# A hybrid gMLP and sparse-attention block on one core: top-k rounds placed elsewhere on VectorE, one low part made by another engine, one softmax behind a split, operands at new addresses

## The chip, the cores and the metric

The kernel runs on one core of one Trainium2 chip. The metric is the device time of one execution in microseconds (us). A core has five engines that run side by side and wait for each other only at semaphores: TensorE (PE in the profile; PEld is its loading of the stationary operand), VectorE (DVE), ScalarE (ACT), GpSimd (POOL) and SyncE (SP), which here only starts DMAs. DMA moves data between main memory and the core's buffer; one kind, started by POOL, adds to what lies at the target.

## The reference

One decoder layer on x of 512 x 1024, all in fp32. The block modulates a normalized x, projects it once, and splits the result:

```python
h = rms_norm(x, norm1_g) * (1.0 + scale1) + shift1
z = h @ w_in     # -> a_u, a_v, q, k, v, qi, ki, wi, g_a, g_b
y_a = chunked_gmlp(gelu(a_u), gelu(a_v), ...)        # mixer A: 128 x 128 causal mixing in 8 groups
score = sum_h wi * relu(qi @ ki.T)                   # indexer, causal
sel_score, sel_idx = lax.top_k(score, 128)           # per query: 128 keys
y_b = attention(q, k, v over the selected keys)      # mixer B: 8 heads, 2 kv heads
merged = sigmoid(g_a) * (y_a @ w_proj_a) + sigmoid(g_b) * (y_b @ w_proj_b)
x = x + gate1 * (merged @ w_out)
x = x + gate2 * swiglu(norm2(x) modulated)           # FFN, then a last RMSNorm
```

## The kernel before

**Products.** Every fp32 product is made of three fp32r matmuls, high·high, high·low and low·high (`mm3`, L53 to L55). So each weight chunk (128 x 1024, 512 KB) that SP streams in as `raw` is split: ScalarE writes its rounded copy `hi` (L128), and the low part `lo` comes in one of two ways. Either VectorE subtracts, raw − hi (L135), or, where the chunk is marked "dma", ScalarE writes the rounded −raw into `lo` (L130) and POOL starts a DMA that adds raw to it (L131). Activations are split in the same way by ScalarE (L379) and VectorE (L380).

**Order.** There is no scheduler: each engine executes its instructions in the order in which the code issues them. The stages are: norm 1 with the k projection and the first q chunks (to 53 us); the rest of q and the indexer's projections (to 109); W_AV, eight steps `vs` (to 160); W_AU, eight steps s = 0 to 7, two chunks W_AU[g][0] and W_AU[g][1] per group g (to 211); then four times a gate unit (`ga_unit(g)`, two steps) and the two chunks of W_PA[g], s = 8 to 23 (to 298); attention, with the chunks of W_GB between its steps (to 384); W_PB, W_O, the FFN.

**Names.** In the W_AU and gate steps `au_tasks` issues what VectorE and ScalarE do beside the matmuls. `mix_mm` forms a mixing product in a PSUM bank `mix`; `mix_a` (L1014, L1017) and `mix_b` (L379, L380) turn it into y and split y. A gate unit multiplies sums and differences of weight and activation blocks (`pga`); the low parts of its weight combinations are subtracted by VectorE (L1088). `part<-pb,sg` (L1185) takes a W_PA product out of PSUM. The row sums L233 (`Gc`) are short side products of other weights. `t_diff_h(n)` forms differences of blocks of the activation, `hraw`, and `t_split_h(n)` splits them; the tables QT and VT say in which step of the q and W_AV stages these are issued, behind the indexer's scores (`idx`, `rl`, `sco`).

**Top-k.** Selecting 128 keys takes 16 rounds for each of three query blocks i = 3, 2, 1 (block 0 has no more than 128 keys). A round is `topk_round(i)`: MAX8 finds the eight largest (L749), MATCH_REPLACE strikes them out (L750); after the sixteenth, `topk_end` (L753) makes the mask. The rows are 512, 384 and 256 wide. The 48 rounds and three ends wait in the list `bg`; `run_bg(us)` adds `us` to a credit and issues rounds while it lasts, each priced at 0.65 + 0.26·i (at most 1.5 is carried over). What an attention unit still needs is issued ahead of its softmax.

**Attention.** A unit u is one query block and one pair of heads; the twelve units go by in steps. In step s, `at_step(s)` issues the product of unit s−3's weights with v (`pv`), the scores of unit s (`qk`), its softmax (`at_soft_a`, L1221 and L1223), the transposes of unit s−2 (`pT`, L1254) with the split of the transposed weights into `th` (ScalarE, L1309) and `tl` (VectorE, L1310), and the second half of the softmax of unit s−1 (L1238, L1240). Unit 8 is the first of block 1; the pool `mid` gives tiles their addresses in the order of their first declaration.

Of the kernel before, what the change touches and what calls it, by code (L numbers as in the profile page):

```python
# [9 lines left out]
F32 = mybir.dt.float32  # L10
# [18 lines left out]
def block_kernel(ctx: ExitStack, tc: tile.TileContext, x, positions, w_ada_t, w_in,  # L29
# [3 lines left out]
    T, V, A, P, SY = nc.tensor, nc.vector, nc.scalar, nc.gpsimd, nc.sync  # L33
# [5 lines left out]
    w_in, w_ffn_in, w_ffn_out = w_in[0], w_ffn_in[0], w_ffn_out[0]  # L39
# [152 lines left out]
    hraw = base.tile([128, 128 + 4096], F32, name="hraw", tag="s2b", bufs=1)  # L192
# [12 lines left out]
        return base.tile([128, 1024], F32R, name=name, tag=f"S2_{k}", bufs=1)[:, :]  # L205
    mid_stack = ExitStack()
    mid = mid_stack.enter_context(tc.tile_pool(name="mid", bufs=1))
    mv = mid.tile([128, 4, 2], F32, name="mv")
    mva = mid.tile([128, 4, 2], F32, name="mva")
    for t in ("v_hi", "v_lo"):  # L210
        mid.tile([128, 1024], F32, name="eraw", tag=t, bufs=1)
    bst = mid.tile([128, 4, 24], F32, name="bst")
    mid.tile([128, 16], F32, name="fill2")
    ffn = []
# [24 lines left out]
    def group(src, c0, n=256, K=8, mods=None, dma=(), where=None, nm=1, mraw="A2"):  # L239
        ids = []  # L240
        for k0 in range(0, K, 4):
            ids.append(add_w(src, list(range(k0, min(K, k0 + 4))), c0, n,
                             "dma" if k0 // 4 in dma else V, where.pop(0) if where else None))
            for _ in range(nm if isinstance(nm, int) else nm[k0 // 4]):
                m = next(mods, None) if mods is not None else None
                if m is not None:
                    add_m(*m, mid=mods is mm_ and mraw)
                    if mraw == "A2" and mods is mm_:
                        stream[-1]["mid"] = ("A2", "G0")[mid2[0] % 2]
                        mid2[0] += 1  # L250
        return ids
# [31 lines left out]
                addm("A2" if k % 4 else "A1")  # L283
    W_AU = []
    for g in range(4):
        W_AU.append(group(w_in, 256 * g, dma=(0, 1) if g else ()))
        if g in (1, 2):
            addm("A2" if g == 1 else "G0")
    W_GA, W_PA = [], []
# [65 lines left out]
    for i in range(4):  # L355
        t = base.tile([128, D], F32, name=f"x{i}", tag=f"X{i}", bufs=1)
# [42 lines left out]
    ch(lambda: V.tensor_scalar(ang, ang, 3.1415925, -3.1415925, op0=OP.min, op1=OP.max))  # L399
    ch(lambda: V.scalar_tensor_tensor(nl, ang, -1.0, ang, op0=OP.mult, op1=OP.max))  # L400
    ch(lambda: V.tensor_scalar(nl, nl, -1.0, math.pi / 2, op0=OP.mult, op1=OP.add))
    sn = mid.tile([128, 4, 128], F32, name="sn", tag="A2", bufs=1)
    tab = {"i": mid.tile([128, 2, S], F32, name="tab_i", tag="G2", bufs=1),
           "q": mid.tile([128, 2, S], F32, name="tab_q", tag="G3", bufs=1)}
# [221 lines left out]
    def q_rope(G):  # L626
        rope_a(("q", G), qpk[G], "q", 128)

    def q_roped(G):
        rope_b(("q", G))  # L630
        for k in range(4):
            h = 4 * G + k
            P.dma_start(qdv[h // 2][0:32, h % 2], qpk[G][32 * k:32 * k + 32].rearrange("p (i n) -> p i n", i=4))
# [23 lines left out]
    k_hi = mid.tile([128, 2, S], F32R, name="k_hi", tag="k_hi", bufs=1)  # L657
# [9 lines left out]
    v_lo = mid.tile([128, 4, 256], F32R, name="v_lo", tag="v_lo", bufs=1)  # L667
    kit = mid.tile([128, 4, 64], F32, name="kit", tag="A1", bufs=1)
    kin = mid.tile([128, 4, 128], F32, name="kin", tag="A2", bufs=1)
    wi = mid.tile([128, 4, 8], F32, name="wi")  # L670
    mid.tile([128, 96], F32, name="fill")
    rki = sm[:, 8:12]

    def ki_stats():
# [93 lines left out]
    def run_bg(us):  # L768
        credit[0] += us
        while bg and credit[0] >= bg[0][0] and iu[1] >= 8 * (4 - bg[0][1]):  # L770
            pop_bg()
        credit[0] = min(credit[0], 1.5)
# [47 lines left out]
    def idx_mms(n):  # L820
        while iu[0] < 24 and n:
            idx_mm(units[iu[0]])
            iu[0] += 1
            n -= 1

    qstep = [0, 0]
    QT = {0: [lambda: k_a(0)],
          1: [lambda: k_a(1), lambda: rope_b(("k", 0))],
# [4 lines left out]
          6: [lambda: qi_b(3, 1), lambda: qi_b(3, 0)],  # L833
          7: [ki_stats, lambda: k_b(0), ki_norm],
          8: [lambda: k_b(1)],
          9: [lambda: q_rope(0)], 10: [lambda: q_roped(0)]}

    def q_tasks():
        s = qstep[0]
# [79 lines left out]

    TH = {}  # L920

    def hblk(kh, th):
        return hraw[:, kh * 2048:(kh + 1) * 2048].rearrange("p (j n) -> p j n", j=4)[:, :, th * 256:(th + 1) * 256]

    def t_diff_h(n):
        b11, b21, b12, b22 = (hblk(kh, th) for th in range(2) for kh in range(2))
        V.tensor_sub(*{1: (b11, b12, b11), 3: (b12, b22, b12), 2: (b22, b22, b11), 4: (b21, b21, b22)}[n])

    def t_split_h(n):
        src = {1: hblk(0, 0), 3: hblk(0, 1), 2: hblk(1, 1), 4: hblk(1, 0)}[n]  # L930
        if n == 3:
            hi = base.tile([128, 4, 256], F32R, name="th_", tag="gate", bufs=1)
            lo = [mid.tile([128, 256], F32R, name="tl_", tag=t, bufs=2) for t in ("qh", "qh", "ql", "ql")]
            A.activation(hi, src, AF.Copy)
            for j in range(4):
                V.tensor_sub(lo[j], src[:, j], f(hi[:, j]))
            TH[3] = ([hi[:, j] for j in range(4)], lo)
        elif n < 4:
            t = [base.tile([128, 4, 256], F32R, name="th_", tag=f"X{2 * n - 2 + e}", bufs=1) for e in range(2)]
            split(*t, src)  # L940
            TH[n] = tuple([t[e][:, j] for j in range(4)] for e in range(2))
        else:
            mid.tile([128, 112], F32, name="fillc")
            hi = mid.tile([128, 4, 256], F32R, name="th_", tag="T4", bufs=1)
            mid.tile([128, 16], F32, name="filld")
            lo = [base.tile([128, 2, 256], F32R, name="tl_", tag="acc", bufs=2) for _ in range(2)]
            A.activation(hi, src, AF.Copy)
            for e in range(2):
                V.tensor_sub(lo[e], src[:, 2 * e:2 * e + 2], f(hi[:, 2 * e:2 * e + 2]))
            TH[4] = ([hi[:, j] for j in range(4)], [lo[j // 2][:, j % 2] for j in range(4)])  # L950

    def hb(kh, th):
        return tuple([s1(8 * e + 4 * kh + j)[:, th * 256:(th + 1) * 256] for j in range(4)] for e in range(2))

    VT = {0: [lambda: t_diff_h(1), lambda: t_diff_h(3)], 1: [lambda: q_rope(1), wn_sums],
          2: [lambda: q_roped(1), lambda: t_diff_h(2)], 3: [lambda: t_split_h(3), lambda: t_diff_h(4)],
          4: [lambda: t_split_h(1), load_bs], 5: [lambda: t_split_h(4)], 6: [lambda: t_split_h(2)], 7: [ws_mask]}
    for i in (3, 2, 1):
        for _ in range(16):
            bg.append((0.65 + 0.26 * i, i, topk_round))  # L960
# [7 lines left out]
    for h in range(2):  # L968
        pb = [bank(b, "pav") for b in range(4)]
        for i in W_AV[h]:  # L970
            idx_accs()
            for fn in VT.get(vs, []):
                fn()
            if vs > 1:
                run_bg(1.2)
            if vs in (5, 6):
                for tk in (2 * vs - 10, 2 * vs - 9):
                    v_stats(tk, 0)
            vs += 1
            hi, lo = get(i)  # L980
            for tk in range(4):
                opt_a_mm(pb[tk], tk, hi, lo, stream[i]["kts"], hT, 8)
            idx_mms(3)
            if vs == 7:
                rows_T()
        for tk in range(4):
            A.activation(vg[tk // 2][:, tk % 2, h * 512:h * 512 + 512], pb[tk], AF.Gelu_apprx_tanh)
# [47 lines left out]
    def au_tasks():  # L1035
        s = austep[0]
        austep[0] += 1
        if s == 0:
            for tk in range(4):
                ln_v(tk)  # L1040
            rstd(rva, mva[:, :, 1], 4)
            V.scalar_tensor_tensor(sm[:, 32:36], mva[:, :, 0], -1.0, rva, op0=OP.mult, op1=OP.mult)
        elif s == 1:
            bias_b()
        if s == 10:
            mix_a(7)
            mix_b(7)
        if s in (6, 10, 14, 18):
            adv(W_GA[(s - 6) // 4][0])
        if s in (7, 11, 15, 19):  # L1050
            ga_b((s - 7) // 4)
        ms = AT.get(s - 1, []) if s < 10 else []
        for m in ms:
            mix_a(m)
        if s > 9:
            run_bg(1.25)
        while dl:
            dl.pop(0)()
        for m in ms:
            mix_b(m)  # L1060
        if 0 < s < 10:
            run_bg(4.0 if s < 6 else 1.25)
        if s == 19:
            at_req(0)
        if s == 22:
            st["stop"] = 1 << 30
# [229 lines left out]
    def at_step(s):  # L1296
        if s >= 3:
            yh, yl, pp = at_pv(s - 3)
            A.activation(yh, pp, AF.Copy)
            V.tensor_sub(yl, pp, f(yh))  # L1300
        if s < NU:
            at_qk(s)
            if s not in (2, 3):
                at_soft_a(s)
            if s == 0:
                at_split(2)
        if 2 <= s <= NU + 1:
            for o, ol, p in at_T(s - 2):
                A.activation(o, p, AF.Copy)  # L1309
                V.tensor_sub(ol, p, f(o))  # L1310
        if s in (2, 3):
            at_soft_a(s)
        if 1 <= s <= NU:
            at_soft_b(s - 1)
        if s < NU:
            at_exp(s)
        if 0 < s < NU - 2 and s != 2:
            at_split(s + 2)
        if 3 < s < 8:
            run_bg(1.0)  # L1320

    for g in range(4):
        ga_unit(g)
# [819 lines left out]
```

## Time and profile before

| what | value |
|---|---|
| runs | 804.96, 804.35, 802.96 us (median 804.35) |
| the profiled execution | 803.53 us; its span 801.5 us |
| mean granted TensorE clock over the span | 0.996 |
| busy: PE, DVE, ACT, POOL | 97%, 84%, 56%, 13% |
| DMA | 148.83 MB, mean 186 GB/s |
| low parts by accumulating DMA | 13, landing 4.4 to 9.6 us after issue |

The span is what the trace covers; the execution's own time is 2 us longer. A busy share is a mean over the whole span. Rows of a timeline give the start in us, the duration, the engine, the line, the operation, output and inputs by the program's names, shapes, and in brackets how long the engine had stood idle before it and which instruction ended that.

### The profile page before, as it was taken

How to read it: one execution, taken by the hardware profiler on the slowest of the kernel's cores; microseconds unless marked ns; L12 is line 12 of the kernel's file. 1: busy time of each engine (PE TensorE's matmuls, PEld its weight loads, DVE VectorE, ACT ScalarE, POOL GpSimd, SP SyncE). 2: the span in 40 equal slices, each digit the busy share in tenths (PEclk: the TensorE clock that was granted, in tenths of full speed). 3: DMA queues.
4: the chain of work that ended last, by engine and by line, in shares of the span. 5: the costliest groups of instructions: out<-in, count | busy, mean ns of one | idle time of the engine just before them, and what ended most of it. 6: DMA issues, size and time to landing. Idle time of an engine off the chain costs nothing.

```text
span 801.5 us, 12714 instructions
## 1 busy us (share of the span) xinstructions
PE 780.9 (97%) x4836; PEld 701.9 (88%) x4836; DVE 675.6 (84%) x1143; ACT 449.2 (56%) x759; POOL 100.9 (13%) x161
## 2 busy tenths in 40 slices
PE   6999999989999999989999999999999999999996
PEld 5789888878889988878888899999999999888886
DVE  6959868987998879997696878899898989887786
ACT  5654556464543365555635577555565556757552
POOL 2082152120000010101000021111111200000001
PEclk9999999999999999999999999999999999999999
DMA  9956487776434443637640608797989876566552
GB/s 356 337 160 176 142 250 228 220 163 182 125 106 132 132 132 112 164 102 260 210 159 1 210 19 211 208 273 229 264 237 245 257 217 168 174 209 190 189 174 105
DMA packets 89485, 148.83 MB, mean 186 GB/s; under 512 B 6992, under 2 KB 56912, under 8 KB 89264
## 3 DMA queue, kind: packets, MB, share of 16 engines
q1 hardware_dynamic: 75056, 106.54, 41.1%
q0 software_dynamic: 12784, 36.97, 19.7%
q10 hardware_dynamic: 1584, 4.50, 1.6%
q8 instruction: 38, 0.62, 0.3%
q14 instruction: 23, 0.19, 0.1%
HBM read 135.80 MB, written 25.17 MB: 201 GB/s over the span
## 4 chain that ended last, share of the span: by engine, by line
PE 61%; issue 13%; DVE 13%; DMA 6%; ACT 4%; POOL 1%; POOLq 0%; DVEq 0%; ACTq 0%
PE R L53 6%; PE R L55 6%; PE R L54 6%; PE pb L55 4%; PE pb L53 4%; PE pb L54 4%; DMA raw<-in_w_ffn_in_dram 3%; PE pfo L54 3%; PE pfo L53 3%; PE pfo L55 3%; PE po L53 2%; PE po L55 2%; PE po L54 2%; PE pgb L53 1%; PE pgb L55 1%
## 5 line engine op out<-in xcount | busy, mean ns | idle before, releaser
L128 ACT ACTIVATE hi<-raw 128x1024 fp32r<-128x1024 f32 (+2 forms) x89 | 92.1, 1039 | 44.9 <-PE pfo L55 18.2
L135 DVE TENSOR_TENSOR lo<-raw,hi 128x1024 fp32r<-128x1024 f32 (+2 forms) x69 | 83.6, 1215 | 31.6 <-ACT hi L128 31.5
L55 PE MATMUL pb<-s,lo 128*128 128x512 f32 (+1 forms) x128 | 48.3, 378 | 2.4 <-DMA lo<-raw 2.4
L54 PE MATMUL pb<-s2b,hi 128*128 128x512 f32 x128 | 49.8, 389 | 0.0
L53 PE MATMUL pb<-s,hi 128*128 128x512 f32 (+1 forms) x128 | 48.6, 379 | 0.0
L54 PE MATMUL pb<-s,hi 128*128 128x512 f32 (+1 forms) x128 | 48.1, 376 | 0.0
L53 PE MATMUL R<-tb,hi 128*128 128x256 f32 x160 | 44.4, 277 | 0.2 <-ACT R L1887 0.2
L53 PE MATMUL R<-tb,sx 128*128 128x256 f32 x160 | 44.3, 277 | 0.2 <-ACT R L1887 0.2
L54 PE MATMUL R<-tb,hi 128*128 128x256 f32 x160 | 44.2, 276 | 0.0
L55 PE MATMUL R<-tb,lo 128*128 128x256 f32 x160 | 44.2, 276 | 0.0
L55 PE MATMUL R<-tb,sx 128*128 128x256 f32 x160 | 44.2, 276 | 0.0
L54 PE MATMUL R<-tb,sx 128*128 128x256 f32 x160 | 44.2, 276 | 0.0
L1446 POOL TENSOR_TENSOR sm<-sm,mhalf 128x1 f32<-128x1 f32 x7 | 5.6, 798 | 222.1 <-DVE sm L1445 217.1
L233 DVE CUSTOM_DVE_ANT_0 mraw<-mraw,cb,cols 128x1024 f32<-128x1024 f32 x24 | 30.9, 1287 | 1.2 <-DMA mraw<-in_w_ada_t_dram 1.2
L53 PEld LDWEIGHTS R<-tb,hi 128*128 128x128 f32 x160 | 30.0, 188 | 0.6 <-ACT R L1887 0.4
L53 PEld LDWEIGHTS R<-tb,sx 128*128 128x128 f32 x160 | 30.0, 188 | 0.4 <-ACT R L1887 0.4
L55 PEld LDWEIGHTS pb<-s,lo 128*128 128x128 f32 x128 | 24.0, 188 | 7.0 <-DMA lo<-raw 3.3
L54 PEld LDWEIGHTS R<-tb,sx 128*128 128x128 f32 x160 | 30.0, 188 | 0.0
L54 PEld LDWEIGHTS R<-tb,hi 128*128 128x128 f32 x160 | 30.0, 188 | 0.0
L55 PEld LDWEIGHTS R<-tb,lo 128*128 128x128 f32 x160 | 30.0, 188 | 0.0
L55 PEld LDWEIGHTS R<-tb,sx 128*128 128x128 f32 x160 | 30.0, 188 | 0.0
L338 POOL DMA_DIRECT2D wsum<-in_w_ffn_out_dram x20 | 17.9, 893 | 96.7 <-DMA wsum<-wsum 55.9
(544 smaller groups left out, 2823.9 us busy)
## 6 DMA issues: line engine op xcount, KB each, us to landing
raw<-in_w_ffn_in_dram SPq DMA_DIRECT2D x44, 512.0 KB, 7.2
raw<-in_w_in_dram SPq DMA_DIRECT2D x40, 512.0 KB, 4.1
wsum<-in_w_ffn_out_dram POOLq DMA_DIRECT2D x30, 512.0 KB, 8.3
raw<-wsum SPq DMA_DIRECT2D x20, 512.0 KB, 3.7
raw<-in_w_ffn_out_dram SPq DMA_DIRECT2D x18, 512.0 KB, 4.6
eraw<-in_w_ada_t_dram SPq DMA_DIRECT2D x16, 512.0 KB, 7.0
mraw<-in_w_ada_t_dram SPq DMA_DIRECT2D x16, 512.0 KB, 5.2
lo<-raw POOLq DMA_DIRECT2D x13, 512.0 KB, 5.8
```

What stands on the lines that cost most here:

```text
L53: T.matmul(o, wh, rh, start=start, stop=False, **kw)
L54: T.matmul(o, wh, rlo, start=False, stop=False, **kw)
L55: T.matmul(o, wlo, rh, start=False, stop=stop, **kw)
L128: A.activation(hi[:, :m], e["raw"][:, :m], AF.Copy)
L135: e["lo"].tensor_sub(lo[:, :m], e["raw"][:, :m], f(hi[:, :m]))
L233: V.tensor_tensor_reduce(out=raw, in0=raw, in1=cb, scale=scale, scalar=add, op0=OP.mult, op1=OP.add, accum_out=dst)
L338: P.dma_start(wsum[n][o], src, accum_op=OP.add)
L1446: P.tensor_tensor(r2[:, tk:tk + 1], r2[:, tk:tk + 1], mhalf[:, :1], op=OP.pow)
```

## The change

1. Tiles of the pool `mid` are declared in another order, so that they lie elsewhere. By bytes within a partition: `v_hi` goes from 144960 to 144896 and `v_lo` from 149056 to 148992; `k_hi` from 198656 to 195008 and `k_lo` from 202752 to 199104; `th` from 178176 to 203200; `tl` and the indexer's keys from 207360 to 207296. Taken within 128 bytes, v now starts at 0 (before 64), `th`, `tl`, k and the indexer's keys at 64 (before 0).
2. The low part of W_AU[1][1] is made by VectorE, not by ScalarE and an accumulating DMA.
3. Two input differences, `t_diff_h(1)` and `t_diff_h(3)`, are issued in the last step of the q stage; the tasks of the W_AV steps that follow move up by one step.
4. The credits of `run_bg` are others: 1.4 for 1.2 in W_AV; 5.5 for 4.0 in s = 1 to 3, 2.0 for 4.0 in s = 4 and 5, 0.6 for 1.25 in s = 8 and 9; from s = 10 on 0.6 in the steps of a gate unit and 2.4 in those of W_PA (0.8 in the last), where it was 1.25 throughout; in attention 0.9 in steps 3 to 7 for 1.0 in steps 4 to 7.
5. Softmax 8 is issued behind the split of unit 6's transposed weights, not ahead of it.

The number of rounds stays 48. The order on TensorE and of SyncE's DMAs stays as it was.

```diff
+    for t in ("v_hi", "v_lo"):
+        mid.tile([128, 1024], F32, name="eraw", tag=t, bufs=1)
     mv = mid.tile([128, 4, 2], F32, name="mv")
     mva = mid.tile([128, 4, 2], F32, name="mva")
-    for t in ("v_hi", "v_lo"):
-        mid.tile([128, 1024], F32, name="eraw", tag=t, bufs=1)
...
+    for t, n in (("G2", 1024), ("G3", 1024), ("P1", 2048)):
+        mid.tile([128, n], F32, name="p0", tag=t, bufs=1)
+    wi = mid.tile([128, 4, 8], F32, name="wi")
+    mid.tile([128, 80], F32, name="fill")
+    for t in ("k_hi", "k_lo", "A2", "A3"):
+        mid.tile([128, 1024], F32, name="p0", tag=t, bufs=1)
...
-        W_AU.append(group(w_in, 256 * g, dma=(0, 1) if g else ()))
+        W_AU.append(group(w_in, 256 * g, dma=((), (0,), (0, 1), (0, 1))[g]))
...
-          9: [lambda: q_rope(0)], 10: [lambda: q_roped(0)]}
+          9: [lambda: q_rope(0)], 10: [lambda: q_roped(0), lambda: t_diff_h(1), lambda: t_diff_h(3)]}
...
-    VT = {0: [lambda: t_diff_h(1), lambda: t_diff_h(3)], 1: [lambda: q_rope(1), wn_sums],
...
+    VT = {0: [lambda: t_diff_h(2)], 1: [lambda: t_split_h(3), lambda: q_rope(1), wn_sums],
...
-                run_bg(1.2)
+                run_bg(1.4)
...
         if s > 9:
-            run_bg(1.25)
+            run_bg(0.6 if s % 4 < 2 else 2.4 if s < 20 else 0.8)
...
         if 0 < s < 10:
-            run_bg(4.0 if s < 6 else 1.25)
+            run_bg(5.5 if s < 4 else 2.0 if s < 6 else 1.25 if s < 8 else 0.6)
...
-            if s not in (2, 3):
+            if s not in (2, 3, 8):
                 at_soft_a(s)
...
-        if s in (2, 3):
+        if s in (2, 3, 8):
             at_soft_a(s)
...
-        if 3 < s < 8:
-            run_bg(1.0)
+        if 2 < s < 8:
+            run_bg(0.9)
```

What this does to the order is seen at three places. A row of the order is the line, the operation, output and inputs; after the change the lines from L206 on stand some lines further down (L1014 is L1019, L749 is L754, L1310 is L1315).

VectorE in W_AU, around the first y, before. `sco_623` are the scores of block 3:

```order
L1014 SCALAR_TENSOR_TENSOR y<-mix,cols,bsb 128x512
L1017 TENSOR_TENSOR y<-y,u 128x512
L380 TENSOR_TENSOR s2b<-y,s2a 128x512
L749 MAX m_1835<-sco_623 128x8
L750 MATCH_REPLACE sco_623<-m_1835,sco_623 128x512
L749 MAX m_1838<-sco_623 128x8
L750 MATCH_REPLACE sco_623<-m_1838,sco_623 128x512
L749 MAX m_1841<-sco_623 128x8
L750 MATCH_REPLACE sco_623<-m_1841,sco_623 128x512
L753 TENSOR_SCALAR sco_623<-sco_623 128x512
L233 ISA mraw,Gc<-mraw,cb,cols 128x1024
```

and after, where `sco_631` is block 3 and `sco_630` block 2:

```order
L758 TENSOR_SCALAR sco_631<-sco_631 128x512
L754 MAX m_1806<-sco_630 128x8
L755 MATCH_REPLACE sco_630<-m_1806,sco_630 128x384
L1019 SCALAR_TENSOR_TENSOR y<-mix,cols,bsb 128x512
L1022 TENSOR_TENSOR y<-y,u 128x512
L380 TENSOR_TENSOR s2b<-y,s2a 128x512
L754 MAX m_1855<-sco_630 128x8
L755 MATCH_REPLACE sco_630<-m_1855,sco_630 128x384
L754 MAX m_1858<-sco_630 128x8
L755 MATCH_REPLACE sco_630<-m_1858,sco_630 128x384
L233 ISA mraw,Gc<-mraw,cb,cols 128x1024
```

Block 3's last rounds and its end moved ahead of the first y, with one round of block 2; between the first y and the second (behind L233) stand two rounds of 384 in place of three of 512 and an end.

VectorE in gate unit 1, from the second weight combination to the third low part, before:

```order
L1097 TENSOR_TENSOR raw<-raw 128x4x128
L749 MAX m_2206<-sco_622 128x8
L750 MATCH_REPLACE sco_622<-m_2206,sco_622 128x384
L1088 TENSOR_TENSOR lo<-raw,hi 128x1024
L749 MAX m_2237<-sco_622 128x8
L750 MATCH_REPLACE sco_622<-m_2237,sco_622 128x384
L1088 TENSOR_TENSOR lo<-raw,hi 128x1024
L1104 TENSOR_TENSOR raw<-raw 128x1024
L1185 TENSOR_TENSOR part_2042<-pb,sg 128x512 x2
L749 MAX m_2291<-sco_622 128x8
L750 MATCH_REPLACE sco_622<-m_2291,sco_622 128x384
L1088 TENSOR_TENSOR lo<-raw,hi 128x1024
```

and after, from the second of the two rounds behind L1102 (before L1097):

```order
L755 MATCH_REPLACE sco_630<-m_2219,sco_630 128x384
L1093 TENSOR_TENSOR lo<-raw,hi 128x1024
L754 MAX m_2250<-sco_630 128x8
L755 MATCH_REPLACE sco_630<-m_2250,sco_630 128x384
L754 MAX m_2253<-sco_630 128x8
L755 MATCH_REPLACE sco_630<-m_2253,sco_630 128x384
L1093 TENSOR_TENSOR lo<-raw,hi 128x1024
L1109 TENSOR_TENSOR raw<-raw 128x1024
L1190 TENSOR_TENSOR part_2055<-pb,sg 128x512 x2
L1093 TENSOR_TENSOR lo<-raw,hi 128x1024
```

The round between `part` and the third low part is gone; the two places ahead hold two rounds each where each held one, so four stand ahead of the third low part in place of three.

VectorE in attention step 8, before (the rounds are those of block 1, `sco_621`):

```order
L1300 TENSOR_TENSOR s2b<-pv,s2a 128x2x128
L749 MAX m_3385<-sco_621 128x8
L750 MATCH_REPLACE sco_621<-m_3385,sco_621 128x256
L749 MAX m_3388<-sco_621 128x8
L750 MATCH_REPLACE sco_621<-m_3388,sco_621 128x256
L749 MAX m_3391<-sco_621 128x8
L750 MATCH_REPLACE sco_621<-m_3391,sco_621 128x256
L749 MAX m_3394<-sco_621 128x8
L750 MATCH_REPLACE sco_621<-m_3394,sco_621 128x256
L753 TENSOR_SCALAR sco_621<-sco_621 128x256
L1221 ISA pt,mx<-qk,sco_621 128x256
```

(two of these L1221, L1223 and then the split L1310 follow) and after:

```order
L1305 TENSOR_TENSOR s2b<-pv,s2a 128x2x128
L1315 TENSOR_TENSOR tl<-pT,th 128x512
L1315 TENSOR_TENSOR tl<-pT,th 128x256
L758 TENSOR_SCALAR sco_629<-sco_629 128x256
L1226 ISA pt,mx<-qk,sco_629 128x256
```

The split stands directly behind the s2b subtraction, the round's end and the softmax behind the split, and the four rounds of this step are issued in earlier steps.

More of the change, by code (lines that the diff above doesn't have):

```diff
@@ L401, in block_kernel @@
     ch(lambda: V.tensor_scalar(nl, nl, -1.0, math.pi / 2, op0=OP.mult, op1=OP.add))
+    for t, n in (("G2", 1024), ("G3", 1024), ("P1", 2048)):
[4 more added lines that the diff above has]
+        mid.tile([128, 1024], F32, name="p0", tag=t, bufs=1)
+    mid.tile([128, 16], F32, name="fill3")
     sn = mid.tile([128, 4, 128], F32, name="sn", tag="A2", bufs=1)
@@ L669, in block_kernel @@
     kin = mid.tile([128, 4, 128], F32, name="kin", tag="A2", bufs=1)
-    wi = mid.tile([128, 4, 8], F32, name="wi")
-    mid.tile([128, 96], F32, name="fill")
     rki = sm[:, 8:12]
@@ L824, in idx_mms, with hblk, t_diff_h @@
             n -= 1
+    def hblk(kh, th):
+        return hraw[:, kh * 2048:(kh + 1) * 2048].rearrange("p (j n) -> p j n", j=4)[:, :, th * 256:(th + 1) * 256]
+    def t_diff_h(n):
+        b11, b21, b12, b22 = (hblk(kh, th) for th in range(2) for kh in range(2))
+        V.tensor_sub(*{1: (b11, b12, b11), 3: (b12, b22, b12), 2: (b22, b22, b11), 4: (b21, b21, b22)}[n])
     qstep = [0, 0]
@@ L920, in block_kernel @@
     TH = {}
[L922 to L927, printed above, removed]
     def t_split_h(n):
@@ L953, in hb @@
         return tuple([s1(8 * e + 4 * kh + j)[:, th * 256:(th + 1) * 256] for j in range(4)] for e in range(2))
-    VT = {0: [lambda: t_diff_h(1), lambda: t_diff_h(3)], 1: [lambda: q_rope(1), wn_sums],
-          2: [lambda: q_roped(1), lambda: t_diff_h(2)], 3: [lambda: t_split_h(3), lambda: t_diff_h(4)],
-          4: [lambda: t_split_h(1), load_bs], 5: [lambda: t_split_h(4)], 6: [lambda: t_split_h(2)], 7: [ws_mask]}
+    VT = {0: [lambda: t_diff_h(2)], 1: [lambda: t_split_h(3), lambda: q_rope(1), wn_sums],
+          2: [lambda: q_roped(1), lambda: t_diff_h(4)], 3: [lambda: t_split_h(1)], 4: [lambda: t_split_h(4), load_bs],
+          5: [lambda: t_split_h(2)], 6: [ws_mask]}
     for i in (3, 2, 1):
```

## The prediction

> **What bounds the kernel.** I read the engines' totals on the profile's page, then TensorE's list of waits, then the timelines around each wait, since a nearly full TensorE leaves only its own pauses to win.
>
> ```profile
> PE 780.9 (97%) x4836; PEld 701.9 (88%) x4836; DVE 675.6 (84%) x1143; ACT 449.2 (56%) x759; POOL 100.9 (13%) x161
> PE pv L54 <- DVE tl L1310: 3.2, 2, 2.9
> PE pb L55 <- DMA lo<-raw: 2.4, 2, 2.0
> PE pT L1254 <- DVE part L1185: 0.7, 1, 0.7
> ```
>
> TensorE is busy 780.9 of 801.5 us of span, so at most some 20 us are pauses. The three wait rows (us in total, times, longest) are those that the change can touch: 6.3 us. The edits take no matmul away. So the gain is these pauses, what hangs on them, and the pace of a few matmuls; the loss is whatever new pause VectorE, at 84%, causes.
>
> The largest pause first. TensorE, VectorE and ScalarE around it (start, duration, instruction, idle before it and who ended it), and two stretches by engine (last columns: granted clock, DMA share, GB/s):
>
> ```profile
> 341.00:345.00 4.00, 1.06 (x6) 0.74 (x5) 3.68 (x14) 1.26 (x5) 0.00 (x0) 0.88 0.01 2
> 345.00:347.50 2.50, 2.50 (x14) 2.50 (x14) 2.50 (x6) 1.48 (x3) 0.55 (x1) 0.51 0.07 15
> ...
> 341.14 0.28 PE L53 MATMUL pv<-th,v_hi 128*128 128x256 f32 x1
> 344.36 0.58 PE L54 MATMUL pv<-tl,v_hi 128*128 128x256 f32 x1 [2.94 <-DVE tl L1310]
> 347.49 0.82 PE L1254 MATMUL pT<-cst,pt 128*128 128x128 f32 x6
> 350.88 0.28 PE L53 MATMUL pv<-th,v_hi 128*128 128x256 f32 x1
> 351.00 0.28 PE L54 MATMUL pv<-tl,v_hi 128*128 128x256 f32 x1
> 352.66 0.60 PE L1254 MATMUL pT<-cst,pt 128*128 128x128 f32 x4
> ...
> 338.35 0.87 ACT L1309 ACTIVATE th<-pT 128x512 fp32r<-128x512 f32 x2 [0.77 <-PE pT L1254]
> 338.37 0.42 DVE L749 MAX8 m<-sco 128x8 f32<-128x256 f32 x1
> 342.29 0.29 DVE L753 TENSOR_SCALAR sco<-sco 128x256 f32<-128x256 f32 x1
> 343.62 1.01 DVE L1310 TENSOR_TENSOR tl<-pT,th 128x512 fp32r<-128x512 f32 x2
> 349.35 1.01 DVE L1310 TENSOR_TENSOR tl<-pT,th 128x512 fp32r<-128x512 f32 x2
> ```
>
> Attention step 9 multiplies unit 6's weights with v. Its first matmul ran at 341.14; the second waited for tl(6), which VectorE wrote only at 343.62: four top-k rounds (338.37 to 342.29, 0.98 us each), the round's end and softmax 8 stood ahead of it. The clock then fell to 0.51 for about 2.5 us. From the first pv matmul to the next transposes the step takes 347.49 − 341.14 = 6.35 us; the same pieces one step on take 352.66 − 350.88 = 1.78. So this place costs 4.57 us: 2.94 of waiting, 1.63 of half clock.
>
> **Softmax 8 behind the split, and no rounds left in that step: 3.8 us.** In the new order tl(6) follows the s2b split at 338.04, with no round between. It then waits for ScalarE's th alone (338.35, 0.87 for both pieces) and is done near 339.7, ahead of 341.14. The 4.57 us go. What is late next is tl(7): from the end L753 of the rounds at 342.29 to tl(7) at 349.35 VectorE's chain is 7.06 us (softmax 8, its reciprocal after ScalarE's exponentials, softmax 9). Tl(6) leaves it, but ran while VectorE would have waited for the exponentials, so I take nothing off. Behind the early tl(6) L753 starts near 339.7, tl(7) near 346.75, its first piece ends some 0.6 us later. TensorE wants it at 351.00 − 4.57 = 346.43. A new pause of up to 0.9 us, and I take 0.75, so 3.8 is left; at best 4.57, at worst 3.0, if the chain is longer by another 0.8. The four rounds are paid in earlier steps, where they belong to the stretches below.
>
> [...]
>
> **Low parts of W_AU: 1.2 us.** TensorE waits twice for the accumulating DMAs that POOL starts:
>
> ```profile
> 169.29 0.88 POOL L131 DMA_DIRECT2D lo<-raw  x1 [3.93 <-ACT lo L130]
> 178.59 0.50 PE L55 MATMUL pb<-s,lo 128*128 128x512 f32 x1 [2.03 <-DMA lo<-raw]
> 199.47 0.87 POOL L131 DMA_DIRECT2D lo<-raw  x1 [9.22 <-ACT lo L130]
> 205.55 0.50 PE L55 MATMUL pb<-s,lo 128*128 128x512 f32 x1 [0.38 <-DMA lo<-raw]
> DMA to landing us min/median/max: 4.4/5.8/9.6
> ...
> 166.63 0.68 DVE L749 MAX8 m<-sco 128x8 f32<-128x512 f32 x1
> 168.13 0.69 DVE L749 MAX8 m<-sco 128x8 f32<-128x512 f32 x1
> 184.81 0.75 DVE L1014 SCALAR_TENSOR_TENSOR y<-mix,cols,bsb 128x512 f32<-128x512 f32 x1 [5.00 <-PE mix L1006]
> 198.13 1.05 ACT L130 ACTIVATE lo<-raw 128x1024 fp32r<-128x1024 f32 x1
> ```
>
> The first wait is for W_AU[1][1], issued at 169.29. VectorE now subtracts it (about 1.2 us, one more on VectorE; one ScalarE pass of 1.05 and one POOL issue of 0.88 fewer). It stands behind four rounds of 1.5 us from 166, so it is done near 173.5, 3 us before its use: 2.03 gone. With the VT work that now runs one step earlier, VectorE reaches the rounds about 0.75 us sooner (an estimate from the order: one difference pair moves into an idle stretch of the step before; if that stretch is full, y0 below is 0.75 later).
>
> VectorE then runs eleven long rounds and one shorter before the first y, where it ran eight: 3 × 1.5 + 1.1 + 1.2 for the subtraction, some 6.9 us more with the round's end, against the 5.0 us that it idled before 184.81 and the 0.75: y0 is 1.3 us later. Nothing but mix banks and y buffers waits for it, and these are used steps later. Behind it one round and the round's end fewer stand ahead of y1 and y2, so those come about 1.25 earlier. With them goes the ScalarE pass L130 at 198.13, and so the DMA of W_AU[3][1]: issued at 198.2 instead of 199.47. TensorE, now 2.03 earlier, wants it at 205.17 − 2.03 = 203.1. With this chunk's own 6.0 us of flight it lands at 204.2: a pause of 1.1. So of 2.03 + 0.38 I keep 1.3, and take off 0.1 for the next paragraph. Bounds: a landing of 4.4 us leaves 2.4; one of 9.6 costs 4.7 and a half clock of 1.63, which makes −3.9 (a rival).
>
> **The gate stage: nothing kept, at best.** Rounds move between the units and the W_PA steps. What TensorE waits for there first is the low part of the third difference (L1088) in units 1, 2 and 3:
>
> ```profile
> 237.69 0.55 DVE L749 MAX8 m<-sco 128x8 f32<-128x384 f32 x1
> 238.81 1.21 DVE L1088 TENSOR_TENSOR lo<-raw,hi 128x1024 fp32r<-128x1024 f32 x1
> 240.08 0.38 PE L55 MATMUL pga<-th__1344,lo 128*128 128x256 f32 x1
> 258.73 1.22 DVE L1088 TENSOR_TENSOR lo<-raw,hi 128x1024 fp32r<-128x1024 f32 x1
> 260.94 0.28 PE L55 MATMUL pga<-th__1344,lo 128*128 128x256 f32 x1
> 278.87 1.23 DVE L1088 TENSOR_TENSOR lo<-raw,hi 128x1024 fp32r<-128x1024 f32 x1
> 281.71 0.28 PE L55 MATMUL pga<-th__1344,lo 128*128 128x256 f32 x1
> ```
>
> It is ready 0.06, 0.99 and 1.61 us ahead. Unit 1 gets one round more ahead of it (238.81 − 237.69 = 1.1 to 1.25 us), but VectorE enters that unit about 1.1 us earlier against TensorE, having two rounds fewer in the last W_AU steps. Unit 2 gets a short round and a round's end more (about 1.0), unit 3 two short ones (1.95, of which the earlier start of the part before it covers some). All three end within 0.2 us of their slack, so I charge 0.1 in all; a few tenths each way are possible, and a full long round uncovered in unit 1 would cost 1.2.
>
> **One round fewer in step 3: 0.9 us.**
>
> ```profile
> 297.27 0.42 DVE L749 MAX8 m<-sco 128x8 f32<-128x256 f32 x1
> 302.19 0.39 PE L54 MATMUL pv<-tl,v_hi 128*128 128x256 f32 x1 [0.27 <-DVE tl L1310]
> 305.05 1.28 DVE L1185 TENSOR_TENSOR part<-pb,sg 128x512 f32<-128x512 f32 x2
> 305.79 1.25 PE L1254 MATMUL pT<-cst,pt 128*128 128x128 f32 x8 [0.69 <-DVE part L1185]
> ```
>
> VectorE runs unbroken from 297.27 to both waits, 0.27 and 0.69. Of the two rounds at the start one is gone, 0.98 us: it covers 0.96 but for the 0.1 by which the matmul's slow restart and TensorE's own earlier arrival matter. Between 0.5 and 1.2.
>
> **New addresses: 0.5 us.** [...]
>
> ```profile
> L53 PE MATMUL R<-tb,hi 128*128 128x256 f32 x160 | 44.4, 277 | 0.2 <-ACT R L1887 0.2
> L55 PE MATMUL pv<-th,v_lo 128*128 128x256 f32 x40 | 11.6, 291 | 0.0
> ```
>
> In the FFN group the two operands lie in different halves of 128 bytes, the moving one in the upper, and one matmul means 277 ns; v·th lies the other way round and means 291 (a few of them at half clock). The change turns the halves for pv, and parts them for the 256-wide qk and idx. At about 4.5 ns for each of 114 pv matmuls at full clock, less for 40 others, I take 0.5; bounds 0 and 0.7. One fewer ScalarE pass and POOL issue, in engines at 56% and 13%, costs and gives nothing further.
>
> **Sum.** 3.8 + 1.2 + 0.9 + 0.5 = 6.4 us. The profiled execution took 803.53 us (span 801.5), so its like comes to 797.1; the median of the runs stands 0.8 above it, at 804.35, and gives 797.9. From the bounds the forecast's own range is 795.3 to 800.5. A difference under 0.3% (2.4 us: 801.9 to 806.8) could not be told from none.
>
> **Rivals.** (A) The accumulating DMA of W_AU[3][1] flies 9 us and not 6, as the one at 169.29 did: TensorE stands 4.7 us and its clock halves (1.63). That is 5.2 worse than my 1.1: 803.1, no change. For it speaks that VectorE is now denser there, and the long flight at 169.29 had rounds all around it. Against it: all issues take 0.9 us, and the median of thirteen landings is 5.8. Chance 0.11. [...]
>
> (B) The pause only moves from unit 6 to unit 7, and the half clock with it: tl(7) comes 3 us late and not 0.75, because softmax 8 is held by its scores or by ScalarE. Then 4.57 − 2.3 − 1.6 leaves 0.7 of 3.8: 801.0. [...] Together 0.10.
>
> (C) Slower: VectorE becomes the bound in the gate stage. Each of the three L1088 above comes late by the same d, three times over. The gains of 6.4 are gone at d = 2.15 us, about two long rounds per unit; at 3 us the clock halves too and it is 3 × 4.6 − 6.4 = 7.4 over: 811.8. The rows give at most 1.2 uncovered in one unit. Chance 0.04.
>
> (D) The change does not do what it says: rounds come back in other places as pauses of the same size, 804. For it: VectorE's busy time stays the same. Against: 5.0 us of idle time before 184.81 are there to take them. Chance 0.05.
>
> **Chances.** Forecast 0.70, A 0.11, B 0.10, C 0.04, D 0.05. Faster by over 0.3%: the forecast, B and a little of what lies between, 0.82; the same: A, most of D and a tail of the forecast, 0.13; slower 0.05. The range is drawn from 795.3, the forecast's bound, to 801.7, which takes in B and leaves A, C and D out.
>
> **What would show it.** Right: no wait for DMA near 176; clock 1.0 throughout 341 to 347 and a pv pause under 1 us one step later; VectorE's idle stretch before the first mix product gone; a wait of about 1 us for the low part of W_AU[3][1]; pv matmuls nearer to 277 ns. Wrong: a half clock anywhere after 100 us, a wait for L1088's successor in units 1 to 3 of over 0.5, or that DMA landing after 9 us.

## The result, and the profile after

The changed kernel took 799.38 us (median of 6 runs, 796.94 to 800.86) beside 804.01 for the one before: a ratio of 0.994, 95% interval 0.9918 to 0.9963. Measured a second time it took 797.24 beside 803.79: 0.9919 (0.9905 to 0.9933). The forecast was 797.9. The profiled execution took 796.94 us with a span of 795.2, against 803.53 and 801.5.

The page's first line and TensorE's list of waits after the change, in the form in which they were shown of before:

```profile
PE 778.9 (98%) x4836; PEld 699.9 (88%) x4836; DVE 677.6 (85%) x1144; ACT 447.6 (56%) x758; POOL 100.3 (13%) x160
...
PE pv L54 <- DVE tl L1315: 0.8, 1, 0.8
PE pga L53 <- ACT pga L1132: 0.7, 1, 0.7
PE pb L55 <- DMA lo<-raw: 0.4, 1, 0.4
PE pav L54 <- DMA lo<-raw: 0.2, 1, 0.2
PE pT L1259 <- DVE part L1190: 0.2, 1, 0.2
```

Of the 6.3 us in the three rows of before, 1.4 are left in the same rows, and two waits are new: one for a DMA in W_AV and one for ScalarE in gate unit 1. The attention steps by stretches, and the rows at which TensorE waits now (`lo` of W_AU[3][1], unit 1, step 10):

```profile
341.00:345.00 4.00, 3.81 (x22) 3.06 (x20) 3.96 (x11) 1.90 (x4) 0.55 (x1) 1.00 0.39 89
345.00:347.50 2.50, 1.85 (x16) 1.85 (x17) 1.95 (x7) 2.46 (x8) 0.22 (x1) 1.00 0.88 316
...
176.51 0.39 PE L55 MATMUL pb<-s,lo 128*128 128x512 f32 x1
203.31 0.50 PE L55 MATMUL pb<-s,lo 128*128 128x512 f32 x1 [0.36 <-DMA lo<-raw]
238.32 0.38 PE L53 MATMUL pga<-th__1238,hi 128*128 128x256 f32 x1 [0.67 <-ACT pga L1132]
304.02 0.55 PE L1259 MATMUL pT<-cst,pt 128*128 128x128 f32 x3 [0.16 <-DVE part L1190]
345.65 0.39 PE L54 MATMUL pv<-tl,v_hi 128*128 128x256 f32 x1 [0.84 <-DVE tl L1315]
```

The clock is 1.00 through 341 to 347.5, where it had been 0.51 for half of that. The matmul that stood 2.03 us for the DMA of W_AU[1][1] (178.59 before) starts at 176.51 without a wait.

TensorE's order is the same in both, so the start of each matmul after, less its start before, tells where time was won (the first column is the time in before):

| place | after − before, us | change there |
|---|---|---|
| 121, in W_AV | −0.24 | −0.38 at the start of the kernel, +0.14 behind it |
| 124, behind a W_AV low part | +0.21 | +0.45, a new wait for a DMA |
| 180, behind W_AU[1][1] | −2.21 | −2.42: −2.3 at this place, −0.1 ahead of it |
| 240, behind the third low part of unit 1 | −1.30 | +0.9, all of it at unit 1 |
| 298, end of the gate stage | −0.74 | +0.56: 0.15 at unit 2, 0.28 at unit 3, the rest in small pieces |
| 306, step 3 | −1.77 | −1.03 |
| 347.5, first transposes behind the pv and qk of step 9 | −6.35 | −4.58 |
| 351.1, pv of unit 7, behind the slow restart | −5.24 | +1.11 |
| end | −6.37 | −1.13, in the FFN |

The last line is not the change's: in the trace of before the FFN had two short waits for ScalarE's `R` (0.3 us in the list, at 577.75 and 645.29; the next matmul came 0.22 us behind each, not 0.11) and one late matmul at 574.59 without a wait in the list, and this trace has none of them. So of the 6.6 us between the two profiled executions about 1.1 is not the change's either.

### The profile page after: what moved, and what is told of

Its sections match the earlier page's. It is cut to its first block, busy times and chain, and to the rows that moved or that the text cites. A ratio compares the mean times of both kernels' runs of the same rounds, so it can differ in the third digit from the quotient of the medians.

```text
span 795.2 us, 12710 instructions
## 1 busy us (share of the span) xinstructions
PE 778.9 (98%) x4836; PEld 699.9 (88%) x4836; DVE 677.6 (85%) x1144; ACT 447.6 (56%) x758; POOL 100.3 (13%) x160
## 4 chain that ended last, share of the span: by engine, by line
PE 80%; DVE 9%; DMA 3%; issue 3%; ACT 2%; POOL 1%; POOLq 0%; DVEq 0%; ACTq 0%; SPq 0%
PE R L55 8%; PE R L53 8%; PE R L54 8%; PE pb L55 5%; PE pb L53 5%; PE pb L54 5%; PE pfo L54 3%; PE pfo L55 3%; PE pfo L53 3%; DMA lo<-raw 2%; PE po L53 2%; PE po L54 2%; PE po L55 2%; PE pgb L53 2%; PE pgb L55 2%
## 5 line engine op out<-in xcount | busy, mean ns | idle before, releaser
L233 DVE CUSTOM_DVE_ANT_0 mraw<-mraw,cb,cols 128x1024 f32<-128x1024 f32 x24 | 30.9, 1288 | 1.6 <-DMA mraw<-in_w_ada_t_dram 1.6
L1236 ACT ACTIVATE pt<-pt,mx 128x512 f32<-128x512 f32 (+3 forms) x32 | 17.7, 556 | 18.6 <-DVE mx L1228 18.6
```

What stands on the lines that cost most here:

```text
L233: V.tensor_tensor_reduce(out=raw, in0=raw, in1=cb, scale=scale, scalar=add, op0=OP.mult, op1=OP.add, accum_out=dst)
L1236: A.activation(pt[e][:, :n], pt[e][:, :n], AF.Exp, scale=SCALE, bias=mx[:, 2 + e:3 + e], accum_out=mx[:, 4 + e:5 + e])
```

## The experiments

Each kernel was timed beside the kernel before on the same chip; that is the second number. All the edits are to the changed kernel unless said otherwise.

**e1, before with the softmax move alone.**

```diff
-            if s not in (2, 3):
+            if s not in (2, 3, 8):
...
-        if s in (2, 3):
+        if s in (2, 3, 8):
```

> Before, with softmax 8 moved behind the split of unit 6 and nothing else. Theory 1 (the gain of the attention stage comes from moving the four rounds out of step 8; the softmax move alone only shifts the wait): the pause of 2.94 us at pv of unit 6 goes, but the four rounds (3.9 us) now stand ahead of softmax 8 and of unit 7's split, which comes about 4.3 us late: a pause of 3 to 5 us one step later and the half clock (about 1.6 us) with it, in all between 2 us faster and 2 us slower than before, 802 to 806. Rival (the move itself is what counts): about 3.8 us faster, 800, and no pause over 1 us at unit 7.

805.18 against 803.52: 1.0016 (1.0 to 1.0031), so no gain. TensorE's waits in steps 9 and 10:

```profile
346.87 0.38 PE L53 MATMUL qk<-k_hi,qh 128*128 128x256 f32 x1 [2.30 <-DVE mx L1221]
348.03 1.01 PE L1254 MATMUL pT<-cst,pt 128*128 128x128 f32 x6 [0.18 <-DVE pt L1240]
352.13 0.35 PE L53 MATMUL pv<-th,v_hi 128*128 128x256 f32 x1 [0.34 <-DVE s2b L1300]
353.52 0.39 PE L54 MATMUL pv<-tl,v_hi 128*128 128x256 f32 x1 [1.03 <-DVE tl L1310]
```

The one wait of 2.94 became four of 3.85 together. I had looked for it at unit 7's split; most of it came earlier, at the qk of step 9, which waits until the late softmax 8 has read the scores. No half clock followed (1.00 over 344 to 347.5 and over 347.5 to 352), and from 340 to 353 the step lost 0.4 us more than before. In W_AU this execution lost 1.8 us more than before, by a longer wait for the same DMA and a half clock with it; the edit changes nothing there:

```profile
179.40 0.79 PE L55 MATMUL pb<-s,lo 128*128 128x512 f32 x1 [2.50 <-DMA lo<-raw]
...
176.90:179.50 2.60, 0.10 (x1) 0.10 (x1) 2.46 (x7) 1.41 (x2) 0.92 (x2) 0.90 1.00 199
179.50:183.00 3.50, 3.50 (x10) 2.80 (x11) 0.64 (x1) 0.00 (x0) 0.00 (x0) 0.59 1.03 172
```


**e2, before with the new credits alone**, all the `run_bg` lines of the diff and nothing else.

> Before, with the new credits of run_bg and nothing else: no round is left in attention step 8, and softmax 8 still stands ahead of unit 6's split. Theory 1: unit 6's low part is ready near 340.6 us by the clock of before, ahead of the 341.4 at which TensorE wants it, and unit 7's near 346.0, ahead of 346.4: no pause at either, 4.6 us gained there and about 1.0 in step 3; the DMA waits of W_AU stay at about 2.4 us; the gate stage gives back little, since TensorE comes later: about 5 us faster than before, 799. Rival (the softmax move is needed): the pause of about 3 us stays, 802 to 803.

797.93 against 803.52: 0.9931 (0.9907 to 0.9954). The first low-part matmul of unit 6 and the DMA wait in W_AU:

```profile
339.98 0.28 PE L54 MATMUL pv<-tl,v_hi 128*128 128x256 f32 x1
178.17 0.50 PE L55 MATMUL pb<-s,lo 128*128 128x512 f32 x1 [2.03 <-DMA lo<-raw]
```

No wait is left at unit 6 or unit 7, although softmax 8 still stands ahead of the split, and the wait at W_AU[1][1] is as it was. Against before, TensorE gains 4.5 us from step 8 to step 10, with no 1.1 to give back. The gate stage gave back 0.8, which I had not expected. The credits by themselves give what the whole change gives, within the intervals.

**e3, without the softmax move.**

```diff
-            if s not in (2, 3, 8):
+            if s not in (2, 3):
...
-        if s in (2, 3, 8):
+        if s in (2, 3):
```

> The changed kernel with softmax 8 put back ahead of the split of unit 6. Theory 1: the pause at unit 6 does not come back (under 0.5 us), and the pause of 0.84 us at unit 7 goes, so 0 to 0.9 us faster than the changed kernel, 5 to 7 us faster than before. Rival: the pause at unit 6 returns, 3 us or more slower than the changed kernel.

796.91: 0.991 (0.9894 to 0.9926). The intervals of this and the changed kernel overlap; the traces tell them apart: no wait comes back at unit 6, the matmul of the wait of 0.84 us starts at 344.51 with none, and there TensorE gains 1.1 us on the changed kernel. The move, which the change needs for nothing once the rounds are gone, costs 1.1 us.

**e4, all tiles at their old addresses** (the declarations in the diff undone).

> The changed kernel with all tiles at their old addresses. Theory 1 (addresses do nothing: the interval from one pv matmul to the next was 117.5 ns before and after): the pauses and the pace of the 256-wide matmuls stay as in the changed kernel, within 0.3 us of it in the trace. Rival (the forecast): pv, qk and idx matmuls 4 to 6 ns slower each, 0.5 us in all.

797.1: 0.9928 (0.9905 to 0.995). The group of a pv matmul in the changed kernel, then in this one:

```profile
L55 PE MATMUL pv<-th,v_lo 128*128 128x256 f32 x40 | 11.2, 281 | 0.0
```

```profile
L55 PE MATMUL pv<-th,v_lo 128*128 128x256 f32 x40 | 11.2, 281 | 0.0
```

The same. qk, idx and pv differ by under 0.3 us in sum, in the other direction if any (the 512-wide qk mean 394 to 395 ns at the new addresses and 389 to 391 at the old). The addresses give nothing.

**e5, W_AU[1][1]'s low part by DMA again** (`dma=(0, 1) if g else ()`).

> The changed kernel with W_AU[1][1]'s low part made by the accumulating DMA again. Theory 2 (behind W_AU VectorE sets the time at which the gate stage runs, so what TensorE gains in W_AU it partly waits for again in gate unit 1): the wait of about 2 us near 176 returns, VectorE is relieved of 1.15 us ahead of unit 1, and the pause of 0.67 us there goes: 0.5 to 1.3 us slower than the changed kernel in the trace behind unit 3. Rival (all of the pause is a loss): 2 us or more slower there.

798.2: 0.9938 (0.9917 to 0.9958). In its trace

```profile
178.93 0.50 PE L55 MATMUL pb<-s,lo 128*128 128x512 f32 x1 [1.35 <-DMA lo<-raw]
```

TensorE loses 1.6 us there against the changed kernel, restart included, and has 1.2 of them back by the end of unit 1: at W_AU[3][1] it has no wait, and at unit 1 one of 0.12 and not 0.67. What stays is 0.4 us, a little under what I expected. So three quarters of the gain at this place were paid back further on.

**e6, the input differences in their old steps** (QT and VT as before).

> The changed kernel with the input differences in their old steps (W_AV instead of the last q step). Theory 2: VectorE reaches the rounds of W_AU about 0.75 us later, and gate unit 1 waits so much longer: the pause of 0.67 us there becomes 1.2 to 1.5, the kernel 0.7 us slower. Rival (the shift is hidden in an idle stretch anyway): unit 1 as in the changed kernel, no difference over 0.2 us.

797.63: 0.9928 (0.9911 to 0.9945), not to be told from the changed kernel. In the trace the cost was there, but not where I put it:

```profile
203.87 0.50 PE L55 MATMUL pb<-s,lo 128*128 128x512 f32 x1 [1.50 <-DMA lo<-raw]
```

Unit 1's wait stayed at 0.62; the later VectorE made the DMA of W_AU[3][1] later (issued at 198.84, not 198.29), and TensorE passes this matmul 0.55 us later than in the changed kernel. The rival, a shift hidden in idle time, doesn't hold either.

**e8, fewer rounds ahead of unit 1's third low part.** The rounds of steps 10 to 23 are issued by a table; two of block 2 and three of block 1 come ahead of `adv` in steps 14 and 18, where VectorE waits for a hi copy:

```diff
+    NB = {10: 1, 11: 1, 13: 1, 14: 1, 15: 1, 17: 2, 18: 2, 19: 2, 21: 1, 22: 1, 23: 1}
...
+        run_n({14: 2, 18: 3}.get(s, 0))
         if s in (6, 10, 14, 18):
...
-            run_bg(0.6 if s % 4 < 2 else 2.4 if s < 20 else 0.8)
+            run_n(NB.get(s, 0))
```

> The changed kernel with the rounds of the gate stage placed otherwise: two of the four rounds ahead of unit 1's third low part are taken away and issued behind unit 1, into the 2.9 us in which VectorE waits for a hi copy, three of block 1 likewise behind unit 2. Theory 2: the pause of 0.67 us at unit 1 and those of 0.1 to 0.2 at the third low parts go, TensorE keeps about 1.3 us more to the end of the gate stage: 1.3 us faster than the changed kernel, 798. Rival (unit 1's wait is ScalarE's own): the pause stays over 0.4 us, no difference.

795.53: 0.99 (0.9883 to 0.9916). ScalarE at unit 1 in the changed kernel (with the VectorE row that it waits for), then here:

```profile
235.08 1.23 DVE L1109 TENSOR_TENSOR raw<-raw 128x1024 f32<-128x1024 f32 x1
236.41 1.06 ACT L1092 ACTIVATE hi<-raw 128x1024 fp32r<-128x1024 f32 x1 [2.51 <-DVE raw L1109]
237.88 0.38 ACT L1132 ACTIVATE pga<-pga 128x256 f32<-128x256 f32 x1
```

```profile
234.38 1.06 ACT L1104 ACTIVATE hi<-raw 128x1024 fp32r<-128x1024 f32 x1 [0.19 <-DVE raw L1121]
236.56 0.37 ACT L1144 ACTIVATE pga<-pga 128x256 f32<-128x256 f32 x1 [0.60 <-PE pga L55]
```

In the first the copy of `pga`, for which TensorE waits, stands on ScalarE behind the hi split, and that waits for VectorE's L1109, which has four rounds ahead of it in this unit where before the change it had two. In the second the copy waits for TensorE. No wait is left at unit 1, and by the end of the gate stage TensorE is 1.3 us ahead of the changed kernel, 1.6 counted from the wait ahead of it.

The copy is not all that held TensorE there. In the changed kernel the third low part of unit 1 and the first matmul that reads it are

```profile
237.50 1.22 DVE L1093 TENSOR_TENSOR lo<-raw,hi 128x1024 fp32r<-128x1024 f32 x1
238.78 0.38 PE L55 MATMUL pga<-th__1238,lo 128*128 128x256 f32 x1
```

The matmul starts 0.06 us after VectorE is done, so without the copy's delay TensorE would have stood for the low part instead. In units 2 and 3 the gap is 0.05 as well (259.63 to 259.68, 280.67 to 280.72), and at unit 1 it is 0.05 or 0.06 in a1 and in e2 to e6. In e8 it is 1.3: VectorE ends at 236.71, the matmul starts at 238.03.

**e10, e8 without the softmax move.**

> As e8_gate, and softmax 8 back ahead of the split of unit 6. Theories 1 and 2 together: neither the pause at unit 1 nor the one at unit 7: about 2 us faster than the changed kernel, 8 us faster than before. Rival: the pauses only move on into the steps behind, no faster than the changed kernel without the softmax move.

794.43: 0.9891 (0.9874 to 0.9909), 9.6 us less than before: the lowest of all; its interval lies below that of the changed kernel's first measurement and overlaps the second by its upper end only. Its largest waits between 16 us and the end are 0.3 (W_AU[3][1]), 0.2 and 0.2.

**a1, the changed kernel again**, for its spread.

> The changed kernel once more, to see its spread. Theory 3: its times fall in two heaps some 3 us apart, and in the trace a slow one differs from a fast one by a stretch of the FFN at 117.8 ns; the pauses at gate unit 1 (0.67) and attention unit 7 (0.84) are there in every one. Rival: no such stretch; the spread lies in DMA waits at the start.

796.52 to 798.05: one heap, and both waits (0.79 at unit 1, 0.83 at unit 7) are there. The two heaps of the first measurement (796.94 and 797.50; 798.69 to 800.86) did not come back.

**e11, a pause put into the FFN of e10** (`for _ in range(7 if q == 5 else 0): A.activation(ps[0], R[3], AF.Copy)` ahead of the copy `R[2], R[1]`). What led to it: the profiled executions of e3 and e4 have a stretch of some 50 us in which the FFN's 256-wide matmuls follow one another at 117.8 ns and not 113.3, and it starts behind a wait for ScalarE. Its start in e3, and the same 40 us in the changed kernel and in e3 (TensorE: busy time, count, clock, DMA share, GB/s):

```profile
533.53 0.38 PE L53 MATMUL R<-tb,hi 128*128 128x256 f32 x1 [0.52 <-ACT R L1892]
```

```profile
540.00:580.00 40.00, 40.00 (x356) 1.00 0.91 249
```

```profile
540.00:580.00 40.00, 40.00 (x342) 1.00 0.90 242
```

> e10_gate_no_soft8 with one pause put into the FFN: in its sixth unit ScalarE repeats a finished copy seven times (the same values again) ahead of the copy that TensorE waits for, which makes TensorE stand for 0.5 to 1 us near 535. Theory 3 (the 256-wide matmuls have two paces, 113.3 and 117.8 ns from one to the next, and a pause can flip them; the address of the operands doesn't matter): after the pause the FFN's matmuls run at 117.8 for some tens of us, so 1.5 to 4 us slower than e10. Rival: the pace stays 113.3 and only the pause is added, 0.5 to 1 us slower.

797.35: 0.9923 (0.9908 to 0.9937).

```profile
561.49 0.38 PE L53 MATMUL R<-tb,sx 128*128 128x256 f32 x1 [1.81 <-ACT R L1906]
```

The pause was longer and later than meant, and the matmuls behind it went on at 113.3 ns. It cost 2.1 us where it stands, restart included; at the end the trace is 1.6 behind e10's, which had lost 0.5 elsewhere. So this pause did not bring the slower pace, and what does stays open. The executions of e3 and e4 with such a stretch took 798.94 and 800.87 us, each the highest of its kernel's six, so the upper heap of the changed kernel's first measurement may be of this kind; that is not shown.

## Why the prediction was right or wrong

The total came out in the range: 6.4 forecast, 4.6 and 6.6 between medians, 6.6 between the two profiled executions. That the last figure is so near is luck. The parts that the prediction named come to 5.3 in the traces (3.5, 0.8, 1.0 and 0), and the 1.1 of the FFN fill the gap.

- **The pause at unit 6, 3.8.** Measured −4.58 and +1.11: 3.5. The new wait at unit 7, for which I took 0.75, is 0.84, and 1.11 with a slow restart, for the reason given: tl(7) at 344.91, behind softmax 8, the exponentials and softmax 9. What I did not ask was which of the two edits in this part does the work. e2 and e3 show it: the credits do all of it, and the softmax move costs 1.1. I put the rounds' leaving and the move under one heading, and so forecast a gain that one of them lessens.
- **Low parts of W_AU, 1.2, with the gate stage at −0.1 inside it.** Measured −2.3, then +0.97 at unit 1 and +0.56 behind it: 0.8. The step that was to take 1.1 of it back took nothing more than before: the DMA of W_AU[3][1] was issued at 198.29 as reckoned (198.2) and was on TensorE's path for 0.36 us, having landed some 1.1 us sooner than the flight of before would give. So TensorE came to unit 1 2.27 us earlier than before and not 1.3, while VectorE's third low part came 1.31 earlier (237.50 for 238.81), and the difference was lost there. "The gate stage: nothing kept" failed in its size for this, 0.1 against 1.5. The two misses nearly cancel for a reason: in unit 1 the end of the third low part sets TensorE's time, wherever TensorE waited ahead of it. What I did not see is a second path from VectorE: the matmuls ahead of that low part wait for a copy of ScalarE that stands in its queue behind a hi split that VectorE feeds, and it came to the same moment. e8 shows the rounds as the cause of both, by taking them away.
- **One round fewer in step 3, 0.9.** Measured 1.03.
- **New addresses, 0.5.** Nothing, by e4. No run shows the 4.5 ns a matmul as an effect of the address. The step that failed is the reading of two groups' means (277 and 291 ns) as such an effect. Without the three matmuls at half clock (415 ns each) the 291 is 281, and the 4 to 5 ns that are left stand at old and new addresses: from start to start, outside waits and the half clock, pv matmuls mean 117.5 ns in before and 117.6 in the changed kernel, those of the FFN's group `R` 113.3 in both. Why the two differ stays open.
- **The rivals.** A's long flight did not come here: TensorE had the low part of W_AU[3][1] 5.0 us after its issue (198.29 to 203.31). B came in small, as forecast; e1 shows a pause that only moves, though without the half clock. C's mechanism, VectorE as the bound of the gate stage, is real and cost 1.5 us in all, under the 6.4 from which it would have decided. Of the softmax move and the addresses alone D's outcome, no gain, is true.
- **The signs.** No wait near 176, the clock at 1.00 and VectorE's idle stretch gone (the first y at 185.96, with no idle time before it) came as said. The wait for W_AU[3][1] was 0.36 and not about 1, pv stayed at 281 ns and not nearer to 277, and the wait of 0.67 at unit 1 is longer than the 0.5 that was named as a sign of being wrong.

## What to carry to other kernels

When a wait has two causes on the same engine, what stands ahead in the queue and in which order, price them apart: moving one instruction past another helps only if what is left behind isn't itself wanted next, and here taking the work out of the step was enough. When a stall is removed ahead of a stage that another engine bounds, look in that stage for every queue that the busy engine feeds, not only for the tile that it writes last: here the wait came back through ScalarE and through that tile at the same moment, and by the rows the cure of one alone would have left the other. And a round of filler belongs where its engine waits for something else: the same 48 rounds in other places gave 5.6 us by themselves (e2), and a further 1.5 when those of the gate stage were moved again (e10 beside e3).

## What the runs showed of the hardware

- TensorE's granted clock fell to half at a wait of 2.94 us (before, up to 344.36: 0.88 over 341 to 345, 0.51 over 345 to 347.5) and at one of 2.50 (e1, up to 179.40: 0.90 over 176.9 to 179.5, 0.59 over 179.5 to 183). It stayed at 1.00 at waits of 2.30 (e1, over 344 to 347.5), 2.03 (before, over 176.5 to 180) and 1.81 (e11, over 559 to 565). Worked out from the 0.88 and the 0.90, the clock fell some 2.6 us into the wait in before and some 2.1 us into it in e1 (estimates), and the wait of 2.30 in e1 passed without a fall. So the length of the wait alone does not tell these apart. What does is not shown, nor whether the 1.63 us of half clock at unit 6 come in every execution of before, of which there is one trace.
- In e3 and in the changed kernel, whose addresses are the same, the FFN's 256-wide matmuls ran at 117.8 and at 113.3 ns from start to start over the same 40 us (342 and 356 of them from 540 to 580), at a clock of 1.00 in both. Over the some 50 us of e3's stretch that is about 2 us, an estimate: 4.5 ns on each of some 425 matmuls.
- POOL's accumulating DMAs all take about 0.9 us to issue and land after very different times; of the changed kernel (the issues' count and durations in ns, then us to landing):

```profile
L131 POOL DMA_DIRECT2D lo<-raw x12: 852/872/966, 105.3 to 319.0; - x12
...
DMA to landing us min/median/max: 4.4/5.2/10.7
```

For the one chunk W_AU[3][1] TensorE had the low part 6.1 us after the issue in before (199.47 to 205.55) and 5.0 in the changed kernel (198.29 to 203.31).
